# A transformer pair on one core: the opening is reordered around blocks of k, and the gate columns ride with the token-major values

## The chip, the cores and the metric

One core of a Trainium2 chip runs the whole program in one launch. The metric is device microseconds of one execution, the median of several runs; lower is better. The engines are named as the profile names them: PE is TensorE (PEld its weight loads), DVE is VectorE, ACT is ScalarE, POOL is GpSimd, SP issues the DMAs.

## The reference

Two blocks follow each other on 512 tokens of 1024 features. The change lies in the first one, and there ahead of and inside the token mixer (cut):

```python
mod = (silu(c) @ ada_w + ada_b)                       # 6 x 1024
sh_t, sc_t, g_t, sh_c, sc_c, g_c = split(mod, 6)
h = rms_norm(x, tm_pre_g) * (1.0 + sc_t) + sh_t
p = split_columns(h @ w_in)     # ml_q ml_k ml_v ml_o ml_i ml_f gla_q gla_k gla_v gla_r gla_a conf sc gate
ml = mlstm_chunked(p["ml_q"], p["ml_k"], p["ml_v"], p["ml_i"] + ml_i_bias, p["ml_f"] + ml_f_bias)
log_a = log_sigmoid(p["gla_a"] @ gla_w_a2 + gla_a_bias) / 16
gl = gla_chunked(p["gla_q"], p["gla_k"], p["gla_v"], log_a)
a, g = split(p["conf"], 2)      # a convolution branch on a * sigmoid(g)
```

Behind it come the convolution branches, the gates that merge four branches, w_o, a convolutional FFN, and the second block (pooling, sparse attention, FFN). All matrix products are wanted at close to f32 precision.

## The kernel before, in words

**Products.** Features lie on the partitions: x0 and h are 8 k-tiles of 128 x 512. A weight block is 128 x 1024 (8 k-tiles of 128 output columns, 512 KB); `wload` fetches it into a raw tile over SP's queue, ScalarE rounds it to float32r (`hi`, L119) and VectorE takes the rest (`lo`, L120). h is held in the same way as a pair, hh and hl. `mm3` makes one product from three matmuls of 512 columns: hi x hh (L131), hi x hl (L132), lo x hh (L133). A gemm of one block is 24 matmuls into a PSUM bank. `gemm_t` turns the sides round (h is the weight, the weight block the moving side) and gives token-major results: 96 matmuls of 256 columns (L157) for 512 tokens of 256 values. Raw, hi and lo tiles have three buffers each, the stage tiles `sraw` four, PSUM has eight banks (three `acc`, two `tp`, and `pa`, `pb`, `pc`).

**Order.** A scheduler at build time sets a static order on each engine; weight loads are lifted ahead by a fixed priority. Engines wait for each other by semaphores.

**Opening (L353 to L447).** c is fetched as a row broadcast to all partitions (cb). A modulation column is one `ada_st` (L347): VectorE multiplies a 128 x 1024 tile of ada_w with cb and sums it. For k = 0 to 7 the scale column 8+k is made, two pieces of x are loaded, squared (L379) and added (L381), and x times its gain, neither normed nor shifted, is split into hh and hl (L394, L395). With these, four blocks (gq0, gq1, gk0, gk1; tiles `wst`) are multiplied as they arrive. When all x is there, the column sum (L240), the root (`rsqrt`, L217 to L233) and four transposes (L247) give rx, which scales the four results (L411, L413). Then the shift columns 0 to 7 follow, seven by `ada_st` and one by TensorE (L422), and h is made anew, normed and shifted (L428 to L430), for the blocks ifa, ca0, cg0, ca1, cg1. ifa holds the columns of the mLSTM gates and of GLA's rank-16 gate, padded to 128. The missing shift of the first four blocks is made up by sixteen matmuls of the shift columns with `wst` (L439, L440) and four small transposes; it enters as `shw` where gq and gk are scaled (L561, L564).

**GLA and mLSTM.** From ifa the gate rows are made (L480 to L491), then GLA's log gates by two plain f32 products (L540), Exp and Ln and a scan; gv is token-major. kf, the decayed keys, are transposed (L574). For each of two head pairs p: copies of gv into a block-diagonal form (L594, 32 in all), key-value products (L596), state updates one after another on VectorE (L604, L606), copies of the states (L610), the attention products in banks pa and pb (L617) with a predicated copy under the causal mask (L619), and the outputs from attention (L624) and state (L629). The gemms of mq, mk and mv are placed in between by the scheduler. mLSTM follows (gate rows L646 to L676, preparations L700 to L706, products from L713 on), then the transposes of values at L775.

Of the kernel before, what the change touches and what calls it, by code (L numbers as in the profile page):

```python
# [38 lines left out]
for _n, _w in VECS:  # L39
# [6 lines left out]
MT1 = ["gq0", "gq1", "gk0", "gk1", "ifa", "ca0", "cg0", "ca1", "cg1", "gv0", "gv1",  # L46
       "mq0", "mq1", "mk0", "mk1", "mv0", "mv1", "gr0", "gr1", "mo0", "mo1",
       "sb0", "sc0", "sx0", "sb1", "sc1", "sx1"]
NST = 8
NF = 4  # L50
XSTEP = (2, 2, 2, 2, 0, 0, 0, 0)
WSTEP = (1, 1, 1, 1, 1, 1, 1, 1)
ADA_PE = (1,)
# [7 lines left out]
def block_kernel(ctx, tc, io, dbg=None):  # L61
# [83 lines left out]
    def gemm_t(srcs, act, out):  # L145

        kn = KT // len(srcs)
        n = 1024 // kn
        for i, src in enumerate(srcs):
            w = [t.rearrange("p (k n) -> p k n", n=n) for t in wload(src)]  # L150
            for b in range(4):
                t = slice(b * 128, (b + 1) * 128)
                for k in range(kn):
                    q = i * kn + k
                    ah, al = act[0][:, q, t], act[1][:, q, t]
                    for m, (a, x_) in enumerate(((ah, w[0]), (ah, w[1]), (al, w[0]))):
                        T.matmul(out[b], a, x_[:, k], start=(q == 0 and m == 0 and b * n % 512 == 0),  # L157
# [181 lines left out]
    with tc.tile_pool(name="st", bufs=1) as st:  # L339
# [11 lines left out]
        nc.sync.dma_start(out=cb, in_=io["c"].broadcast_to([128, D]))  # L353
        nc.sync.dma_start(out=vec[:, 0:VSTART], in_=io["vec"][:, 0:VSTART])
        A.activation(cb, cb, AF.Silu)
# [4 lines left out]
        wstf = [st.tile([128, NF, 1024], F32R, name=f"wst{n}") for n in range(2)]  # L360
        wst = [(wstf[0][:, m], wstf[1][:, m]) for m in range(NF)]
        wst += [(m4(f"whi{m}", F32R)[:, 0:1024], m4(f"wlo{m}", F32R)[:, 0:1024]) for m in range(NF, NST - 3)]
        accs = [bank(t) for t in ("acc", "acc", "acc", "pa", "pb", "pc", "tp")]
        done = [0] * NST
        ready = 0

        def steps(ms, act, j):
            for m in ms:
                for k in range(done[m], j + 1):
                    sl = slice(k * 128, (k + 1) * 128)  # L370
                    mm3(accs[m], wst[m][0][:, sl], wst[m][1][:, sl], act[0][:, k], act[1][:, k], k == 0, k == KT - 1)
# [1136 lines left out]
```

## Time and profile before

| | |
|---|---|
| median of 3 runs | 1603.59 us (1602.0 to 1603.7) |
| profiled execution | 1603.05 us |
| its span in the trace | 1601.3 us |
| TensorE busy | 1568.9 us (98%) |
| VectorE busy | 1083.4 us (68%) |
| ScalarE busy | 677.5 us (42%) |
| DMA, mean over the span | 110 GB/s, 175.91 MB |

The span is what lies between the first and the last instruction of the trace; the 1.8 us beside it are the start and the end of the execution. Matmuls overlap in the array, so a matmul's own duration (0.39 us for 512 columns) is longer than the time from one start to the next; costs are taken from starts. The granted clock is given as a part of the full 2.4 GHz: 0.50 is 1.2 GHz.

### The profile page before, as it was taken

The page shows a single profiled execution, that of the slowest core. Times are in us where ns is not written, and L with a number is a line of the kernel's source. Part 1 is how long each engine was busy: PE and PEld are TensorE (multiplying, and loading weights), DVE is VectorE, ACT ScalarE, POOL GpSimd, SP SyncE. Part 2 cuts the span into 40 slices and gives each one's busy share as a digit, 9 for nine tenths or more (in the row PEclk, how much of TensorE's full clock was granted, in tenths as well). Part 3 has the DMA queues.
Part 4 walks back from the last instruction along what each step waited for, and adds up shares of the span by engine and source line. Part 5 has one row for each costly group of instructions (what it writes and reads, how often), then busy time and mean ns, then how long its engine had stood idle before and what let it go on. Part 6 is the DMA issues. An engine that isn't in the chain of part 4 may idle for free.

```text
span 1601.3 us, 20852 instructions
## 1 busy us (share of the span) xinstructions
PE 1568.9 (98%) x8015; PEld 1316.4 (82%) x8015; DVE 1083.4 (68%) x2066; ACT 677.5 (42%) x1040; POOL 15.9 (1%) x43
## 2 busy tenths in 40 slices
PE   6999999999999999999999999999999999999997
PEld 4777888888889888888899978888889988888886
DVE  7786897657778865665358899977556565665234
ACT  4456432223463544443244463448343444444122
POOL 0000100000000000000000000000000000000000
PEclk9999999999999999999999999999999999999999
DMA  8411335554550223233345222220241232232331
GB/s 305 170 53 67 106 115 187 184 170 153 177 169 17 79 97 100 92 100 91 96 134 187 75 66 89 83 93 27 79 152 59 80 100 98 92 104 81 98 113 53
DMA packets 50963, 175.91 MB, mean 110 GB/s; under 512 B 5920, under 2 KB 6192, under 8 KB 50864
## 3 DMA queue, kind: packets, MB, share of 16 engines
q1 hardware_dynamic: 50864, 174.58, 33.3%
q8 instruction: 63, 1.03, 0.3%
q14 instruction: 36, 0.29, 0.1%
HBM read 172.46 MB, written 2.10 MB: 109 GB/s over the span
## 4 chain that ended last, share of the span: by engine, by line
PE 90%; DVE 5%; ACT 3%; DMA 1%; issue 1%; SPq 0%; ACTq 0%; DVEq 0%
PE acc L131 23%; PE acc L132 23%; PE acc L133 23%; PE acc L197 3%; PE acc L1340 3%; PE tp L1340 2%; PE pc L1250 1%; PE pa L197 1%; PE pc L197 1%; PE pb L197 1%; PE pb L1340 1%; PE pa L1340 1%; PE pc L1340 1%; DVE lo L120 1%; PE acc L157 1%
## 5 line engine op out<-in xcount | busy, mean ns | idle before, releaser
L120 DVE TENSOR_TENSOR lo<-raw,hi 128x1024 fp32r<-128x1024 f32 (+1 forms) x245 | 296.4, 1211 | 312.0 <-ACT hi L119 307.9
L131 PE MATMUL acc<-hh,hi 128*128 128x512 f32 x1208 | 474.3, 393 | 0.0
L133 PE MATMUL acc<-hh,lo 128*128 128x512 f32 x1208 | 473.1, 392 | 0.0
L132 PE MATMUL acc<-hl,hi 128*128 128x512 f32 x1208 | 473.1, 392 | 0.0
L119 ACT ACTIVATE hi<-raw 128x1024 fp32r<-128x1024 f32 (+1 forms) x245 | 257.1, 1050 | 471.1 <-PE acc L132 352.6
L131 PEld LDWEIGHTS acc<-hh,hi 128*128 128x128 f32 x1208 | 227.7, 189 | 48.9 <-issue 2.0
L132 PEld LDWEIGHTS acc<-hl,hi 128*128 128x128 f32 x1208 | 227.5, 188 | 48.6 <-issue 1.8
L133 PEld LDWEIGHTS acc<-hh,lo 128*128 128x128 f32 x1208 | 227.6, 188 | 47.5 <-issue 0.7
L131 PE MATMUL acc<-act_h,hi 128*128 128x256 f32 (+1 forms) x242 | 80.4, 332 | 0.0
L132 PE MATMUL acc<-act_l,hi 128*128 128x256 f32 (+1 forms) x242 | 80.2, 331 | 0.0
L133 PE MATMUL acc<-act_h,lo 128*128 128x256 f32 (+1 forms) x242 | 80.2, 331 | 0.0
L119 ACT ACTIVATE act_h<-ffe 128x512 fp32r<-128x512 f32 x44 | 27.7, 630 | 102.5 <-DVE ffe L968 102.5
L265 DVE SCALAR_TENSOR_TENSOR raw<-raw,cb 128x1024 f32<-128x1024 f32 x32 | 39.1, 1223 | 40.0 <-DMA raw<-in_ada_dram 40.0
L964 DVE SCALAR_TENSOR_TENSOR ffe<-acc,vec,ffe 128x510 f32<-128x510 f32 x82 | 61.2, 748 | 2.6
L967 ACT ACTIVATE ffe<-ffe 128x512 f32<-128x512 f32 x44 | 27.8, 631 | 79.5 <-DVE ffe L964 79.5
L962 DVE SCALAR_TENSOR_TENSOR ffe<-acc,vec,ffe 128x511 f32<-128x511 f32 x82 | 60.7, 742 | 0.0
L131 PEld LDWEIGHTS acc<-act_h,hi 128*128 128x128 f32 x242 | 46.0, 190 | 4.4
L133 PEld LDWEIGHTS acc<-act_h,lo 128*128 128x128 f32 x242 | 46.0, 190 | 4.3
L132 PEld LDWEIGHTS acc<-act_l,hi 128*128 128x128 f32 x242 | 46.0, 190 | 4.3
L120 DVE TENSOR_TENSOR act_l<-ffe,act_h 128x512 fp32r<-128x512 f32 x44 | 30.3, 690 | 26.5 <-ACT act_h L119 26.5
L808 DVE SCALAR_TENSOR_TENSOR cv<-u,vec,cv 128x512 f32<-128x512 f32 x60 | 43.8, 746 | 0.1
L197 PE MATMUL acc<-hl,hi 128*128 128x256 f32 x144 | 40.2, 285 | 0.0
(632 smaller groups left out, 2778.4 us busy)
## 6 DMA issues: line engine op xcount, KB each, us to landing
raw<-in_up_dram SPq DMA_DIRECT2D x88, 512.0 KB, 3.3
raw<-in_wg_dram SPq DMA_DIRECT2D x48, 512.0 KB, 3.3
raw<-in_dn_dram SPq DMA_DIRECT2D x44, 512.0 KB, 3.5
raw<-in_w_dram SPq DMA_DIRECT2D x43, 512.0 KB, 3.4
raw<-in_ada_dram SPq DMA_DIRECT2D x32, 512.0 KB, 3.4
sraw<-in_ada_dram SPq DMA_DIRECT2D x16, 512.0 KB, 5.3
raw<-in_wo_dram SPq DMA_DIRECT2D x16, 512.0 KB, 3.3
raw<-in_dn_dram SPq DMA_DIRECT2D x11, 384.0 KB, 3.2
```

What stands on the lines that cost most here:

```text
L119: A.activation(hi, src, AF.Copy)
L120: V.tensor_sub(lo, src, hi.bitcast(F32))
L131: T.matmul(out, wh_, ah, start=start, stop=False)
L132: T.matmul(out, wh_, al, start=False, stop=False)
L133: T.matmul(out, wl_, ah, start=False, stop=stop)
L197: T.matmul(a, w_, x_, start=(k == 0 and n == 0 and half == 0), stop=(k == KT - 1 and n == 2 and half == 1), skip_group_check=True)
L265: V.scalar_tensor_tensor(raw, raw, 1.0, cb, op0=ALU.mult, op1=ALU.mult, accum_out=mod[:, i:i + 1])
L808: V.scalar_tensor_tensor(cv[:, j], u0[:, j, k:k + 512], htap[:, 2 * k + j:2 * k + j + 1], cv[:, j], op0=ALU.mult, op1=ALU.add)
L962: V.scalar_tensor_tensor(t[:, 1:512], acc[:, 0:511], vcol(taps, 44 + i), t[:, 1:512], op0=ALU.mult, op1=ALU.add)
L964: V.scalar_tensor_tensor(t[:, 2:512], acc[:, 0:510], vcol(taps, i), t[:, 2:512], op0=ALU.mult, op1=ALU.add)
L967: A.activation(e[0], e[0], AF.Silu)
L1340: T.matmul(o, act[a][:, k, t], w[:, n0:n1], start=(k == 0 and i == 0), stop=(k == KF - 1 and i == 2), skip_group_check=True)
```

## The change

All of x is loaded first. cb is made on the chip: the silu of c as eight columns, each spread by a transpose. Matmuls without a use (`warm`) stand ahead of the first product. rx is made before any product. Then a single loop runs over k: it makes the scale and the shift column of that k, h of that k, and fetches one weight block that holds the k-tile of eight column blocks (gq0, gq1, gk0, gk1, ca0, cg0, ca1, cg1), each with a PSUM bank of its own. No shift is repaired later. The ifa block is gone: its 24 columns stand behind the 256 of gv, so `gemm_t` now has 280 columns, and the gate columns are copied out (gt4) and transposed. The gates' Exp and Ln run once over 128 x 1536. mq and mk are computed ahead of GLA. In GLA both value copies of a group stand ahead of its products, the attention products alternate between the halves of the array's rows, and the outputs are written as two loops.

```diff
-MT1 = ["gq0", "gq1", "gk0", "gk1", "ifa", "ca0", "cg0", "ca1", "cg1", "gv0", "gv1",
+MT1 = ["gq0", "gq1", "gk0", "gk1", "ca0", "cg0", "ca1", "cg1", "mq0", "mq1", "mk0", "mk1", "mv0", "mv1",
...
+NGV = 280
+WW = 1120
+WARM = (3, 12)
...
+        for j in range(KT):
+            nc.sync.dma_start(out=x0[:, j], in_=io["xT"][:, j])
+
+        zero = st.tile([128, 256], F32, name="zero")
+        G.memset(zero, 0.0)
+        idle = bank("acc")
+
+        def warm(n, x_):
+            for _ in range(n):
+                T.matmul(idle[:, 0:x_.shape[1]], ident if x_ is not zero else zero[:, 0:128], x_, start=True, stop=True)
+
+        warm(WARM[0], zero)
...
+        for n in range(2):
+            cp = bank(("pb", "pc")[n])
+            for k in range(4):
+                T.transpose(cp[:, k * 128:(k + 1) * 128], ccol[:, 4 * n + k:4 * n + k + 1].to_broadcast([128, 128]), ident)
...
+        warm(WARM[1], zero)
...
+        colsum(pc, [ssx])
+        warm(2, ssx)
+        V.tensor_copy(s0, pc[:, 0:4])
+        rx = st.tile([128, 512], F32, name="rx")
+        A.activation(rx, rowcast(rsqrt(s0, 1.0 / D, 4)), AF.Copy)
+        warm(2, rx)
+
+        accs = [bank(t) for t in ("acc", "acc", "acc", "pc", "pa", "pb", "tp", "tp")]
         for j in range(KT):
+            g, sh = gcols[:, 0, j:j + 1], mod[:, j:j + 1]
             ada_st(8 + j)
+            ada_st(j)
+            floor[0] = tc.cur_priority
+            w = wload(io["w1"][j])
...
+            V.scalar_tensor_tensor(t, x0[:, j], g, rx, op0=ALU.mult, op1=ALU.mult)
             A.activation(h[0][:, j], t, AF.Identity, bias=sh)
             V.scalar_tensor_tensor(h[1][:, j], t, sh, h[0][:, j].bitcast(F32), op0=ALU.add, op1=ALU.subtract)
...
+            for m in range(NST):
+                sl = slice(m * 128, (m + 1) * 128)
+                mm3(accs[m], w[0][:, sl], w[1][:, sl], h[0][:, j], h[1][:, j], j == 0, j == KT - 1)
...
+        out = [bank(t) for t in ("acc", "acc", "acc", "pc")]
+        gemm_t([io["wgv"][n] for n in range(2)], h, [o[:, 0:NGV] for o in out], NGV)
+        for b in range(4):
+            V.tensor_copy(gt4[:, b, 0:64].rearrange("p (g c) -> p g c", c=32)[:, :, 0:4],
+                          out[b][:, 256:264].rearrange("p (g c) -> p g c", c=4))
+            V.tensor_copy(gt4[:, b, 64:80], out[b][:, 264:280])
+            A.activation(gv[:, b], out[b][:, 0:256], AF.Copy)
+        ifa = bank("tp")
+        for b in range(4):
+            T.transpose(ifa[0:80, b * 128:(b + 1) * 128], gt4[:, b], ident)
...
+        A.activation(rows[:, 2:5], rows[:, 2:5], AF.Exp, scale=-1.0)
+        A.activation(rows[:, 2:5], rows[:, 2:5], AF.Ln, bias=1.0)
...
+        for dst, nm in ((mq, "mq"), (mk, "mk")):
+            for j in range(2):
+                A.activation(dst[:, j], acc_of(f"{nm}{j}"), AF.Copy)
...
+            atp = [bank("pa"), bank("pb")]
+            for b in range(4):
+                t = slice(b * 128, (b + 1) * 128)
+                for hh in range(2):
+                    r = slice(64 * hh, 64 * hh + 64)
+                    T.matmul(atp[hh][:, t], gk[r, p, t], gq[r, p, t])
```

Where the instructions stand now is seen in the orders. First TensorE's queue at the very start. Before, it begins with products (`wst_109` and `wst_110` are the hi and lo halves of the first weight blocks):

```order
L131 MATMUL acc<-hh,wst_109 128x512
L132 MATMUL acc<-hl,wst_109 128x512
L133 MATMUL acc<-hh,wst_110 128x512
```

And now (`zero`, `ssx` and `rx` as moving or weight side mark the matmuls without a use; `cst` is the identity or the ones; L237 is the column sum, L244 the transposes that spread rx):

```order
L358 MATMUL acc<-zero 128x256 x5
L369 MATMUL pb<-cst,ccol 128x128 x4
L369 MATMUL pc<-cst,ccol 128x128 x4
L358 MATMUL acc<-zero 128x256 x10
L237 MATMUL tp<-cst,ssx 128x1 x4
L358 MATMUL acc<-ssx,cst 128x512 x2
L244 MATMUL tp<-cst,rs_y 128x128 x4
L358 MATMUL acc<-rx,cst 128x512 x2
L129 MATMUL acc<-hh,hi 128x512 x3
```

The products moved behind the column sum and the spread of rx, and fifteen zero matmuls and the spread of c stand ahead of those.

Next VectorE's queue in the changed kernel at the same place (L381 adds the squares, L371 copies half of cb, L385 takes the column sum, L344 is `ada_st`, L214 to L230 are the root, L118 is lo, L400 and L402 are nt and hl):

```order
L371 COPY cb<-pc 128x512
L381 TENSOR_TENSOR ssx<-ssx,sq 128x512 x6
L385 COPY s_90<-tp 128x4
L344 SCALAR_TENSOR_TENSOR sraw,mod<-sraw,cb 128x1024
L214 TENSOR_SCALAR rs_s<-s_90 128x4
L397 SCALAR_TENSOR_TENSOR gcols<-mod,scb_120,vec 128x1
L215 TENSOR_SCALAR rs_i<-rs_s 128x4
L216 TENSOR_SCALAR rs_y<-rs_i 128x4
L344 SCALAR_TENSOR_TENSOR sraw,mod<-sraw,cb 128x1024
L228 TENSOR_TENSOR rs_u<-rs_y 128x4
```

The first two modulation sums stand inside the root of rx; before, the first of them stood at the head of the queue and the root came after four of them.

Last TensorE's queue where GLA begins. Before (L617 attention, L574 transposes of kf, L596 key-value products; L131 to L133 are gemms of mq and mk):

```order
L617 MATMUL pa<-e_97 128x128 x4
L617 MATMUL pb<-e_97 128x128
L574 MATMUL tp<-cst,e_97 128x128 x4
L617 MATMUL pb<-e_97 128x128 x3
L133 MATMUL acc<-hh,lo 128x512
L574 MATMUL tp<-cst,e_97 128x128 x4
L596 MATMUL pc<-x1a,e_97 64x256 x2
L131 MATMUL acc<-hh,hi 128x512
L132 MATMUL acc<-hl,hi 128x512
```

And now (L548 transposes of kf, L590 attention, L569 key-value products, L154 the token-major gemm of mv):

```order
L548 MATMUL tp<-cst,e_97 128x128 x8
L590 MATMUL pa<-e_97 128x128
L590 MATMUL pb<-e_97 128x128
L590 MATMUL pa<-e_97 128x128
L590 MATMUL pb<-e_97 128x128
L590 MATMUL pa<-e_97 128x128
L569 MATMUL pc<-x1a,e_97 64x256 x4
L590 MATMUL pb<-e_97 128x128
L590 MATMUL pa<-e_97 128x128
L590 MATMUL pb<-e_97 128x128
L154 MATMUL acc<-hi,hh 128x256
```

Both transposes now stand ahead of the first attention product, and what is mixed with GLA is the gemm of mv alone; those of mq and mk stand ahead of L548.

## Rows read from the trace of the kernel before

**Rows 1.** The page: TensorE's row of the busy times (busy us, share of the span, instructions), and the chain of work that ended last, by engine.

```profile
PE 1568.9 (98%) x8015; PEld 1316.4 (82%) x8015; DVE 1083.4 (68%) x2066; ACT 677.5 (42%) x1040; POOL 15.9 (1%) x43
...
PE 90%; DVE 5%; ACT 3%; DMA 1%; issue 1%; SPq 0%; ACTq 0%; DVEq 0%
```

**Rows 2.** The table by stage, core 0. Columns: the stretch in us from the span's start, its length, busy us and instructions of each engine, the granted TensorE clock as a part of full speed (PEclk), the DMA engines' busy share and GB/s. (The clock's record begins at 20.0 us.)

```profile
11.46:20.10 8.64, 6.58 (x12) 3.55 (x12) 8.27 (x13) 4.88 (x8) 0.00 (x0) 1.00 1.04 403
...
97.80:101.90 4.10, 1.78 (x15) 1.39 (x14) 4.10 (x9) 3.25 (x7) 0.00 (x0) 1.00 0.36 128
101.90:108.70 6.80, 6.80 (x24) 4.18 (x23) 5.24 (x15) 1.19 (x2) 0.00 (x0) 0.50 0.23 77
...
141.50:197.70 56.20, 55.80 (x347) 49.57 (x343) 46.52 (x92) 35.81 (x80) 5.60 (x16) 1.00 0.30 98
197.70:250.00 52.30, 52.30 (x235) 43.29 (x235) 52.05 (x82) 17.28 (x23) 0.00 (x0) 1.00 0.41 130
```

**Rows 3.** The timeline of the opening, VectorE and TensorE: start us, us, engine, line, operation, out<-in, shapes, count, and in brackets the idle time of the engine before it with what ended it.

```profile
5.25 0.17 DVE L359 TENSOR_SCALAR scb<-vec 128x8 f32<-128x8 f32 x1 [5.25 <-DMA vec<-in_vec_dram]
...
7.64 1.23 DVE L347 SCALAR_TENSOR_TENSOR sraw<-sraw,cb 128x1024 f32<-128x1024 f32 x1 [2.22 <-DMA sraw<-in_ada_dram]
...
8.79 0.08 DVE L347 DVE_READ_ACCUMULATOR sraw<-sraw,cb 128x1 f32 x1
...
11.46 0.80 PE L131 MATMUL acc<-hh,wst 128*128 128x512 f32 x1 [11.46 <-ACT wst L119]
```

**Rows 4.** The timeline of TensorE, same columns: 512-column matmuls of the opening and of a later stretch. The distance between the starts is what one costs.

```profile
17.16 0.63 PE L131 MATMUL acc<-hh,wst 128*128 128x512 f32 x1
...
19.29 0.63 PE L133 MATMUL acc<-hh,wst 128*128 128x512 f32 x1
...
53.66 0.39 PE L131 MATMUL acc<-hh,hi 128*128 128x512 f32 x1
...
69.08 0.39 PE L133 MATMUL acc<-hh,lo 128*128 128x512 f32 x1
```

**Rows 5.** The timeline of TensorE, same columns: the column sum, the shift column made by TensorE, the first shift repair matmul and the first row behind the sixteen, the two products of the gate factor, the first of the 96 token-major matmuls and the first row behind them.

```profile
25.03 1.02 PE L240 MATMUL tp<-cst,ssx 128*128 128x1 f32 x8 [0.77 <-DVE ssx L381]
...
44.43 1.84 PE L422 MATMUL tp<-ccol,sraw 128*128 128x1 f32 x16
...
69.30 0.40 PE L439 MATMUL tp<-wst,sh 128*2 128x512 f32 x1
...
72.98 0.39 PE L131 MATMUL acc<-hh,hi 128*128 128x512 f32 x1
...
79.08 1.98 PE L540 MATMUL tp<-rows,wa 16*128 16x512 f32 x4
80.99 0.39 PE L157 MATMUL acc<-hi,hh 128*128 128x256 f32 x1
...
92.61 0.40 PE L131 MATMUL acc<-hh,hi 128*128 128x512 f32 x1
```

**Rows 6.** Groups of instructions by line and shape, VectorE from 0 to 70 us and then ScalarE from 0 to 160 us: line, engine, operation, names, shapes, count | busy us, mean ns of one | idle before them and what ended it.

```profile
L347 DVE SCALAR_TENSOR_TENSOR sraw<-sraw,cb 128x1024 f32<-128x1024 f32 x15 | 18.3, 1219 | 2.2 <-DMA sraw<-in_ada_dram 2.2
L120 DVE TENSOR_TENSOR lo<-raw,hi 128x1024 fp32r<-128x1024 f32 x5 | 6.0, 1221 | 3.9 <-ACT hi L119 3.9
L430 DVE SCALAR_TENSOR_TENSOR hl<-nt,mod,hh 128x512 fp32r<-128x512 f32 x8 | 6.0, 750 | 0.8 <-ACT hh L429 0.8
...
L232 DVE SCALAR_TENSOR_TENSOR rs_u<-rs_u,rs_s 128x4 f32<-128x4 f32 x3 | 0.5, 158 | 0.0
...
L119 ACT ACTIVATE hi<-raw 128x1024 fp32r<-128x1024 f32 x15 | 15.7, 1052 | 25.2 <-PE acc L132 16.6 <-DMA raw<-in_w_dram 4.9 <-PE pc L132 3.4
L429 ACT ACTIVATE hh<-nt,mod 128x512 fp32r<-128x512 f32 x8 | 5.8, 723 | 10.9 <-DVE nt L428 10.3 <-DVE sh L120 0.5
...
L610 ACT ACTIVATE x1a<-x1a 64x960 f32<-64x960 f32 x4 | 4.0, 1003 | 1.3 <-DVE x1a L606 1.2
```

**Rows 7.** The same view, VectorE from 100 to 160 us: the state updates of GLA, the copies of its values (one of 32 stands before 100) and the predicated copies of one of its two halves.

```profile
L606 DVE SCALAR_TENSOR_TENSOR x1a<-x1a,fcol,pc 128x64 f32<-128x64 f32 x28 | 7.8, 278 | 1.4 <-PE pc L596 0.8
...
L594 DVE COPY x1a<-gv 32x128 f32<-32x128 f32 x31 | 6.8, 218 | 2.5 <-PE pc L596 1.8
...
L619 DVE COPY_PREDICATED x2a<-x2a,pa 128x512 f32<-128x512 int32 x2 | 1.5, 739 | 0.9 <-PE tp L624 0.9
```

**Rows 8.** The timeline, columns as in Rows 3: the first of the mLSTM gate rows on VectorE and the row behind the last; the first key-value matmuls of GLA, its last run of outputs and the first row behind it; the last preparation for mLSTM on ScalarE; the first row behind the values of mLSTM; the first transposes of the values of the gated branches.

```profile
83.94 1.36 DVE L646 TENSOR_TENSOR_SCAN rows<-x2a,rows 4x128 f32<-4x128 f32 x4
...
91.42 1.21 DVE L120 TENSOR_TENSOR lo<-raw,hi 128x1024 fp32r<-128x1024 f32 x1
...
105.31 1.12 PE L596 MATMUL pc<-x1a,e 128*64 128x256 f32 x4
...
138.30 0.42 PE L629 MATMUL tp<-x1a,e 128*32 128x128 f32 x6
...
141.48 0.50 PE L132 MATMUL acc<-hl,hi 128*128 128x512 f32 x1
...
154.39 0.62 ACT L706 ACTIVATE mql<-mql 64x512 fp32r<-64x512 f32 x1
...
154.25 0.40 PE L713 MATMUL pc<-mx,sel 128*128 128x512 f32 x1
...
197.72 0.98 PE L775 MATMUL tp<-cst,mv 128*128 128x128 f32 x7
```

More of the change, by code (lines that the diff above doesn't have):

```diff
@@ L156, in gemm_t @@
                     for m, (a, x_) in enumerate(((ah, w[0]), (ah, w[1]), (al, w[0]))):
-                        T.matmul(out[b], a, x_[:, k], start=(q == 0 and m == 0 and b * n % 512 == 0),
+                        T.matmul(out[b], a, x_[:, k], start=(q == 0 and m == 0 and b % (512 // n) == 0),
                                  stop=(q == KT - 1 and m == 2), skip_group_check=True)
@@ L429, in block_kernel @@
             A.activation(h[0][:, j], t, AF.Identity, bias=sh)
             V.scalar_tensor_tensor(h[1][:, j], t, sh, h[0][:, j].bitcast(F32), op0=ALU.add, op1=ALU.subtract)
-            if j not in (KT - 3, KT - 2):
-                steps(range(NF, NST), h, j)
-        shs = sm.tile([128, KT, 2], F32R, tag="sh", name="sh", bufs=1)
-        split(shs[:, :, 0], shs[:, :, 1], mod[:, 0:KT])
-        shp = bank("tp")
-        for j in range(KT):
-            wk = [wstf[n].rearrange("p m (k c) -> p m k c", k=KT)[:, :, j] for n in range(2)]
-            T.matmul(shp[0:2], shs[:, j], wk[0], start=(j == 0), stop=False, skip_group_check=True)
-            T.matmul(shp[0:1], shs[:, j, 0:1], wk[1], start=False, stop=(j == KT - 1), skip_group_check=True)
@@ L441, in block_kernel @@
-        shr = st.tile([128, 512], F32, tag="nt", name="shr", bufs=2)[0:2]
-        A.activation(shr, shp[0:2], AF.Copy)
-        tp = bank("tp")
-        for m in range(NF):
-            T.transpose(tp[:, 2 * m:2 * m + 2], shr[:, m * 128:(m + 1) * 128], ident[0:2, 0:2])
-        shw = sm.tile([128, NF], F32, tag="shw", name="shw", bufs=1)
-        V.tensor_reduce(shw, tp[:, 0:2 * NF].rearrange("p (m n) -> p m n", n=2), axis=AX.X, op=ALU.add)
+            if j == 4:
+                load_consts()
@@ new lines, in block_kernel @@
+        ifa = bank("tp")
+        for b in range(4):
+            T.transpose(ifa[0:80, b * 128:(b + 1) * 128], gt4[:, b], ident)
+        gx, fm, fa = (rows[:, n] for n in range(3))
+        gf = gx[32:36]
+        i_sb, b_sb, d_sb = (rows[0:4, n] for n in range(3))
+        fb = vec[32:36, VOFF["if_bias"]:VOFF["if_bias"] + 1]
+        A.activation(gx[64:80], ifa[64:80], AF.Copy)
+        A.activation(fa[32:36], ifa[32:36], AF.Abs, bias=fb)
+        V.tensor_scalar(gf, ifa[32:36], fb, 0.0, op0=ALU.add, op1=ALU.min)
@@ new lines, in block_kernel @@
+        A.activation(i_sb, ifa[0:4], AF.Identity, bias=vec[0:4, VOFF["if_bias"]:VOFF["if_bias"] + 1])
+        gab = rows[:, 3:5]
+        gmn = m4("gmn")[:, 0:1024].rearrange("p (j t) -> p j t", j=2)
+        for j in range(2):
+            u = bank(("pa", "pb")[j])
+            T.matmul(u, wa2[64:80, j * 128:(j + 1) * 128], gx[64:80])
+            A.activation(gab[:, j], u, AF.Abs, bias=vcol("gla_a_bias", j))
+            V.tensor_scalar(gmn[:, j], u, vcol("gla_a_bias", j), 0.0, op0=ALU.add, op1=ALU.min)
@@ L625, in block_kernel @@
                              start=(b == 0 and hh == 0), stop=False, skip_group_check=True)
+            for b in range(4):
                 for c in range(4):
@@ L1169, in block_kernel @@
         pump(PUMP_V0)
-        gemm_t([io["w2"][m + n] for n in range(4)], h, vb)
+        gemm_t([io["w2"][m + n] for n in range(4)], h, vb, 512)
         for b in range(4):
```

191 lines of the change are left out of this document (50 added, 141 removed).

## The prediction

> **What bounds the kernel now.** I first read the page's busy times and its chain of waits: TensorE is busy for 98% of the span and carries 90% of the chain [rows 1]. The reader should see that almost any TensorE work taken out, or any TensorE gap closed, is time won, and that nothing else is. Next I read the table by stage [rows 2], because a mean hides the stage that is changed. From 141.5 to 197.7 TensorE is busy for 55.80 of 56.20 us and afterwards without a break; VectorE is nearly full from 197.7 to 250 (52.05 of 52.30) but there TensorE still never waits. Before 141.5 there are holes: the first product starts at 11.46 [rows 3], 2.3 us are idle between 97.8 and 101.9, and from 101.90 the granted clock is 0.50 for 6.80 us. Last I read single TensorE rows for the rate [rows 4]: 68 intervals from 53.66 to 69.08 give 0.227 us per 512-column matmul at the full clock, five from 17.16 to 19.29 give 0.426. So the opening runs at half rate; the clock column shows 1.00 there, but the pitch says 1.2 GHz, and I trust the pitch.
>
> The place where both kernels can be compared is the first of the transposes at L775, at 197.72 [rows 8]. Behind it the two orders are the same on every engine, except that the changed kernel has already issued seven 512-column matmuls (7 x 0.227 = 1.6 us) that the old one still has before it. I therefore work out when the changed kernel gets there.
>
> **The change, part by part.**
>
> *Work removed and added on TensorE* [rows 5]. The ifa block goes: 24 x 0.227 = 5.4 us. The shift repair at L439/L440 goes: 69.30 to 72.98, 3.7. L422's sixteen matmuls go: 1.8. The gate columns now ride with the token-major values: the old 96 matmuls of 256 columns took 11.62 us (80.99 to 92.61), 0.121 each. 280 columns are not in the trace; from below they cost 0.121, from above 280/512 of a slower pitch, say 0.14; between 256 columns at 0.121 and 512 at 0.227 the line gives 0.131, and I take 0.130: 96 x 0.130 = 12.5, 0.9 more than now. Four transposes of the gate columns add 0.5. Net 9.5 us less work. The rest of the sum is waiting.
>
> *Opening.* Now products start at 11.46 on an x that is normed later. In the changed order no product starts before the norm factor rx. TensorE issues five zero matmuls, eight transposes of c, ten zero matmuls, then the column sum. Plain f32 is not float32r: two 16x512 products at L540 took 1.91 us [rows 5], so 0.24 per pass of 512 columns and some 0.48 for a 256-column zero matmul, twice that at half rate. Five at half rate from about 1.3 and ten at full rate, with the transposes between them, end at about 12.1; if the clock stays low for longer, at 15.8. vec lands at 5.2 [rows 3]; behind it cst, eight x pieces (2 MB), two ada tiles and a weight tile (1.5 MB) stream at 403 GB/s [rows 2]: x complete near 9, ada 8 at 10.3, ada 0 at 11.6, weights at 12.9. The transfers are then ahead of TensorE's queue. Column sum 1.0 (L240, [rows 5]): 13.1. VectorE then has ada 8 (1.2), twelve small steps of the root (0.16 each, 0.20 apart since each needs the last), ada 0 between them (1.2) [rows 6]: 17.9. Four transposes and the copy of rx: 19.4, where TensorE does its two rx matmuls (1.9) while it would wait anyway. Then lo, ada and nt are queued: nt ends at 21.0, hh takes 0.72 [rows 6], and the first product is at **21.8**. Bounds: 20.0 if ada 8 lies beside the column sum and lo beside the root, 25.5 if the zero matmuls run at half rate. Between 13 and 20 TensorE does little; the old kernel shows 0.50 after such a hole (101.90, [rows 2]), where 6.80 us cost 3.4. I charge 1.5, bounds 0 and 4.
>
> The Trainium skill (TensorE: Matmul & The Clock Gate, Part 1 and Part 4) says that the throttled state is the default, that activity releases it, and that transposes do not count as activity in the same way. The half pitch until 19.29 agrees with the first half of that; no row separates the second. By it the column sum and the rx transposes would bridge nothing, and the loop would pay nearer the upper bound of 4 than my 1.5, which would make the sum some 1593.
>
> *The loop over k.* Eight steps of 24 matmuls: 192 x 0.227 = 43.6. VectorE needs per step two ada sums and one lo (1.22 each), nt and hl (0.75 each, taken alike) and 0.3 of small ones: 5.4 by durations [rows 6], but the next instruction starts before one ends (an ada sum of 1.23 begun at 7.64 is followed at 8.79, [rows 3]), so with 0.08 less for each of the five 5.0 us against TensorE's 5.4; the transfers need 1.5 MB / 403 GB/s = 3.9. All lie beside it, with 0.4 us to spare a step; if the overlaps fail, VectorE paces the loop at about the same 5.4. ScalarE has hi 1.05 and hh 0.72 [rows 6]. Loop end: 21.8 + 43.6 + 1.5 = 66.9.
>
> *Values, gates, mq and mk.* 12.5 + 0.7 (transposes and a short wait) + 1.9 (the two L540 products) + 96 x 0.227 = 21.8 for mq and mk, which stand ahead of GLA now: 103.8. The gate chain on ScalarE and VectorE (table loads, one wide Exp and Ln, scans, four products) starts at 82 and gives the second kf near 102.5 by its rows' durations, so it hides behind mq/mk with 1.3 us to spare. If it slips, TensorE waits as it did before 101.9.
>
> *GLA.* The old kernel spread mq, mk and their products through GLA; now only the 96 matmuls of mv (11.5) remain to fill it. From the first L596 at 105.31 to the last L629 at 141.48 the old one took 36.2 us [rows 8]. In the new order VectorE, after kf, first does the mLSTM gate rows, which took 7.5 us (83.94 to 91.42, [rows 8]): it is free at about 109.3 for the 32 value copies (7.0), 28 state updates (7.8) with two first copies at much the same price (0.5), four predicated copies (3.0) and two lo (2.4) [rows 6, 7], plus an estimated 0.03 between 62 short ones (1.9): 22.5, so 131.8. Exposed behind it: one L596 group 1.0 [rows 8], the sd copy 1.0, and the output's last matmuls 3.2 (138.30 to 141.48). GLA ends at 137.0. Own work in these 33.2 us is about 27.5, so 5.7 are waits. I add 1.0 for a stretch at half clock, since 101.90 to 108.70 cost 3.4 where GLA began with waits: **138.0**. Bounds 133 (waits halved) and 144 (the old 36.2 from about 108).
>
> *mLSTM up to the transposes.* The old kernel still had mk and mv from 141.48 to 154.25 and then 43.5 us to 197.72 [rows 8]. The new one has only those 43.5, the seven matmuls (1.6), and a wait: ScalarE's sixteen preparations of mq and mk, 0.62 each, or 10 us, had mv as their cover and the last of them stands at 154.39 [rows 8]; that cover is gone. Most can now start inside GLA, since mq and mk are there at 104, and I estimate 2.2 left (bounds 0 and 8). 138.0 + 43.5 + 1.6 + 2.2 = 185.3.
>
> **Sum.** 197.72 - 185.3 = 12.4 us earlier. Behind L775 TensorE was never idle up to 250 [rows 2], so it carries the whole gain to the end if weights come as early as now. The profiled execution took 1603.05, within 0.6 of the median 1603.59: 1603.05 - 12.4 = **1590.6**.
>
> **Rivals.**
> *GLA uncovered.* The old chain's 36.2 us stay although the filler is gone: end 144 instead of 138, gain 6.4, 1596.7. For it: each of the four L596 groups waits for VectorE's copies, and the updates wait for it. Against it: part of the old 36.2 was gemm work put in between. 20%.
> *Late opening.* Zero matmuls at half rate: first product 25.5, gain 8.7, 1594.4. For it: the old opening stays at half rate for 8 us. 10%.
> *Few stalls.* Opening at 20.0 (1.8), no clock loss (1.5 + 1.0), GLA waits halved (2.9), no mLSTM wait (2.2): 9.4 more, gain 21.8, 1581.3. 20%.
> *Given back.* VectorE, with 52.05 of 52.30 busy from 197.7 to 250, paces the weights when TensorE arrives 12 us sooner with the same list behind it: about 1603. Against it: TensorE has no idle time there now, and the list is only shifted as a whole. 6%.
> *Slower.* TensorE stays at the lower clock in the k loop because each step waits for hh or hl a little, as in the old opening. A step at 0.426 costs 24 x 0.199 = 4.8 us more. Beyond 12.4/4.8 = 2.6 steps the kernel loses, at four of the eight it takes 12.4 - 19.1 = 6.7 us longer, 1609.8. For it: 0.4 us of VectorE's slack a step is little. Against it: once the old kernel ran without gaps (53.66 on) it kept the full rate. 6%. The Trainium skill has this pattern in the same page's section "HAM oscillation — how this bites in real kernels": a loop whose steps each end in a wait starts each step throttled.
>
> **How the numbers follow.** The forecast itself, 1586 to 1595, has 38%. A measurement can tell about 0.2%, 3.2 us. The four faster cases hold 88%, from which I take 2 for a GLA that eats all: faster 0.86; same 0.07 (given back, and that); slower 0.07 (the clock, and some unseen wait). Below 1580 lie about 8% (few stalls, all bounds), above 1600 about 12%: the range is 1580 to 1600.
>
> **What would show it.** First L129 product near 21.8 at a pitch of 0.227; loop end near 67 with 24 matmuls in 5.4 us; 280 columns at 0.130; kf before mk ends; the last L602 near 138; the first L748 transpose near 185. A granted clock of 0.5 in the loop, a gap ahead of L548 or a GLA beyond 144 would make the prediction wrong, and so would a stretch behind L748 that is longer than the old one from L775.

## The result, and the profile after

The change made the kernel slower: 1624.26 us (1623.31 to 1625.27) against 1603.55 for the kernel before on the same chip, a ratio of 1.0142 [1.013, 1.0154]. The forecast was 1590.6, with 1600 as its upper end.

The page of the changed kernel, the rows that answer to [rows 1]:

```profile
PE 1592.1 (98%) x8005; PEld 1325.4 (82%) x8005; DVE 1077.3 (66%) x2060; ACT 666.9 (41%) x1027; POOL 17.2 (1%) x46
...
PE 92%; DVE 5%; ACT 2%; issue 1%; DMA 0%; SPq 0%; ACTq 0%; DVEq 0%
```

TensorE has ten instructions less than before and is busy for 23.2 us more. So the loss is not a wait: the same instructions take longer. The timeline of TensorE after the change (columns as in [rows 3]): the matmuls on rx that have no use and the first product behind them, the first token-major matmuls, the product of the gate factor, the kf transposes, a wait in GLA, the last run of GLA's outputs and the row behind it, a wait in the tail of mLSTM, the transposes of the values of the gated branches, the last product. (A plain f32 matmul stands in the trace as two: the two on rx show as x4.)

```profile
20.71 3.68 PE L358 MATMUL acc<-rx,cst 128*128 128x512 f32 x4 [0.69 <-ACT rx L387]
23.43 1.64 PE L129 MATMUL acc<-hh,hi 128*128 128x512 f32 x3
...
68.73 0.29 PE L154 MATMUL acc<-hi,hh 128*128 128x280 f32 x1
68.86 0.29 PE L154 MATMUL acc<-lo,hh 128*128 128x280 f32 x1
...
83.33 1.12 PE L487 MATMUL pa<-rows,wa 16*128 16x512 f32 x2
...
105.99 1.04 PE L548 MATMUL tp<-cst,e 128*128 128x128 f32 x8
...
116.05 0.44 PE L596 MATMUL tp<-gv,x2a 128*128 128x64 f32 x2 [4.07 <-DVE x2a L592]
...
143.69 1.07 PE L602 MATMUL tp<-x1a,e 128*32 128x128 f32 x30
144.69 0.50 PE L686 MATMUL pc<-mx,sel 128*128 128x512 f32 x1
...
185.21 0.80 PE L129 MATMUL acc<-hh,hi 128*128 128x512 f32 x1 [6.25 <-ACT tmp L734]
...
187.93 0.46 PE L129 MATMUL acc<-hh,hi 128*128 128x512 f32 x1
...
196.80 1.09 PE L748 MATMUL tp<-cst,mv 128*128 128x128 f32 x8 [0.96 <-DVE mv L726]
...
1613.32 0.39 PE L1313 MATMUL tp<-hi,act_l 128*128 128x512 f32 x1
```

The last product in the trace of the kernel before:

```profile
1592.75 0.39 PE L1340 MATMUL tp<-hi,act_l 128*128 128x512 f32 x1
```

At the transposes the change is 0.9 us ahead (196.80 against 197.72 [rows 8]), though it has seven products more behind them than the old kernel; at the last product it is 20.6 us behind. The table by stage shows what happens in between, in a stretch where both do nothing but 512-column products at full clock. First the kernel before, then the changed one, with three of its early stages (columns as in [rows 2]):

```profile
560.00:740.00 180.00, 180.00 (x796) 149.05 (x795) 110.94 (x135) 74.82 (x99) 0.00 (x0) 1.00 0.30 96
```

```profile
23.00:67.00 44.00, 44.00 (x187) 35.22 (x186) 36.73 (x71) 16.32 (x22) 3.92 (x11) 0.99 0.70 241
...
116.00:132.00 16.00, 15.95 (x76) 13.45 (x76) 6.90 (x23) 2.00 (x2) 0.00 (x0) 0.57 0.00 0
...
175.00:200.00 25.00, 17.79 (x85) 14.36 (x85) 24.44 (x50) 9.38 (x16) 0.00 (x0) 0.86 0.40 127
560.00:740.00 180.00, 180.00 (x778) 146.38 (x777) 108.81 (x132) 72.76 (x97) 0.00 (x0) 1.00 0.28 94
```

In the same 180 us, without an idle moment and with a granted clock of 1.00 in both, TensorE issues 778 products instead of 796: 0.2314 us each instead of 0.2261, from one start to the next (the pitch of the texts below). The page counts 3 x 1216 such products; times 0.0053 that is 19.3 us, nearly all of the loss. The other rows show two more things: a half clock in GLA (0.57) behind a wait of 4.1 us, and a wait of 6.3 us before 185.21.

**A line of the diff that the prediction did not price** explains the rate: `WW = 1120`. To hold the block of 280 columns, raw, hi and lo became 4480 bytes wide in each partition instead of 4096, and they stay so for the whole program. 4480 is not a multiple of 256. The compiled programs place the tiles at these bytes of a partition (remainders modulo 256 in brackets):

```
         before                               after
hi       23520 27616 31712   (224 224 224)    24576 29056 33536   (  0 128   0)
lo       35808 39904 44000   (224 224 224)    38016 42496 46976   (128   0 128)
hh, hl   48096, 64480        (224, 224)       51456, 67840        (  0,   0)
```

hi and lo are the weight side of a product, hh and hl its moving side. Before, all agree modulo 256; after, some weight tiles lie 128 bytes off. Theory A: a product costs more where its two sides disagree. Its rivals: wider tiles cost by their width, or the new order behind L748 is slower of itself.

### The profile page after: what moved, and what is told of

Read it like the earlier page. It is cut to its first block, busy times and chain, and to the rows that moved or that the text cites. A ratio compares the mean times of both kernels' runs of the same rounds, so it can differ in the third digit from the quotient of the medians.

```text
span 1621.6 us, 20813 instructions
## 1 busy us (share of the span) xinstructions
PE 1592.1 (98%) x8005; PEld 1325.4 (82%) x8005; DVE 1077.3 (66%) x2060; ACT 666.9 (41%) x1027; POOL 17.2 (1%) x46
## 4 chain that ended last, share of the span: by engine, by line
PE 92%; DVE 5%; ACT 2%; issue 1%; DMA 0%; SPq 0%; ACTq 0%; DVEq 0%
PE acc L130 23%; PE acc L131 23%; PE acc L129 22%; PE acc L194 3%; PE acc L1313 3%; PE acc L154 2%; PE tp L1313 2%; PE pc L1223 1%; PE pa L194 1%; PE pc L194 1%; PE pb L194 1%; PE pa L1313 1%; PE pc L1313 1%; PE pb L1313 1%; DVE lo L118 1%
## 5 line engine op out<-in xcount | busy, mean ns | idle before, releaser
L118 DVE TENSOR_TENSOR lo<-raw,hi 128x1024 fp32r<-128x1024 f32 (+2 forms) x249 | 301.6, 1212 | 353.1 <-ACT hi L117 348.1
L131 PE MATMUL acc<-hh,lo 128*128 128x512 f32 x1216 | 483.7, 398 | 0.0
L130 PE MATMUL acc<-hl,hi 128*128 128x512 f32 x1216 | 482.4, 397 | 0.0
L117 ACT ACTIVATE hi<-raw 128x1024 fp32r<-128x1024 f32 (+2 forms) x249 | 261.4, 1050 | 481.1 <-PE acc L130 334.1
L129 PEld LDWEIGHTS acc<-hh,hi 128*128 128x128 f32 x1216 | 231.7, 191 | 60.5 <-ACT tmp L734 6.6
L131 PEld LDWEIGHTS acc<-hh,lo 128*128 128x128 f32 x1216 | 228.7, 188 | 49.9 <-issue 0.2
L131 PE MATMUL acc<-act_h,lo 128*128 128x256 f32 (+1 forms) x242 | 81.0, 335 | 0.0
L131 PEld LDWEIGHTS acc<-act_h,lo 128*128 128x128 f32 x242 | 45.6, 188 | 4.5
L118 DVE TENSOR_TENSOR act_l<-ffe,act_h 128x512 fp32r<-128x512 f32 x44 | 30.4, 690 | 26.6 <-ACT act_h L117 26.6
L194 PE MATMUL acc<-hl,hi 128*128 128x256 f32 x144 | 40.2, 284 | 0.0
```

Source lines behind the costliest of these rows:

```text
L117: A.activation(hi, src, AF.Copy)
L118: V.tensor_sub(lo, src, hi.bitcast(F32))
L129: T.matmul(out, wh_, ah, start=start, stop=False)
L130: T.matmul(out, wh_, al, start=False, stop=False)
L131: T.matmul(out, wl_, ah, start=False, stop=stop)
L194: T.matmul(a, w_, x_, start=(k == 0 and n == 0 and half == 0), stop=(k == KT - 1 and n == 2 and half == 1), skip_group_check=True)
```

## Experiments

**Addresses mended, the change otherwise whole.**

```diff
-WW = 1120
+WW = 1152
```

(The weight block in memory keeps its 1120 columns.) 1152 columns are 4608 bytes, 18 x 256. Here and below the second time, and what a ratio refers to, is the kernel before on the same chip.

> The changed kernel with one number altered: raw, hi and lo tiles 1152 wide instead of 1120, so 4608 bytes a partition instead of 4480; the order on every engine is the same. Theory A (address step): in the changed kernel a hi, lo or activation tile no longer starts at the same place modulo 256 bytes as its partners, and each 512-column matmul then costs 0.232 instead of 0.227 us; at 4608 bytes all tiles agree again, some 5,300 matmuls get 4.5 ns back, and the time falls from 1624.3 to 1599, the pitch of hi x hl to 0.227. Theory B (the reordered opening or the longer activity slows TensorE for the rest): time stays near 1624, pitch 0.232.

Measured: 1603.33 against 1601.36, 1.0014 [1.0005, 1.0024]. The table by stage and the timeline of TensorE in this kernel:

```profile
116.00:132.00 16.00, 16.00 (x96) 13.34 (x99) 6.85 (x28) 2.00 (x2) 0.00 (x0) 0.63 0.00 1
...
560.00:740.00 180.00, 180.00 (x796) 149.05 (x795) 110.96 (x135) 74.84 (x99) 0.00 (x0) 1.00 0.29 96
```

```profile
66.91 0.29 PE L154 MATMUL acc<-hi,hh 128*128 128x280 f32 x1
...
81.48 1.12 PE L487 MATMUL pa<-rows,wa 16*128 16x512 f32 x2
...
103.70 1.03 PE L548 MATMUL tp<-cst,e 128*128 128x128 f32 x8
...
142.87 0.50 PE L686 MATMUL pc<-mx,sel 128*128 128x512 f32 x1
...
183.37 0.79 PE L129 MATMUL acc<-hh,hi 128*128 128x512 f32 x1 [6.24 <-ACT tmp L734]
...
189.08 0.46 PE L130 MATMUL acc<-hl,hi 128*128 128x512 f32 x1
...
195.13 1.09 PE L748 MATMUL tp<-cst,mv 128*128 128x128 f32 x8
```

The 796 products are back, and with them some 20.5 us of the 25 expected (1.0142 to 1.0014): width alone costs nothing, since these tiles are wider still. What remains is that the change gains nothing where 12.4 us were forecast. That is a second question, taken up below.

**The kernel before, with the address spoiled or kept in three ways.** Tiles of 4480 bytes; 128 bytes put between the weight tiles and the activations; tiles of 4352 bytes, which is 17 x 256 and so agrees modulo 256 but not modulo 512.

```diff
-        raw = wr.tile([128, 1024], F32, tag="raw", name="raw")
+        raw = wr.tile([128, 1120], F32, tag="raw", name="raw")
...
-            hi = wh.tile([128, 1024], F32R, tag="hi", name="hi")[:, :n]
-            lo = wl.tile([128, 1024], F32R, tag="lo", name="lo")[:, :n]
+            hi = wh.tile([128, 1120], F32R, tag="hi", name="hi")[:, :n]
+            lo = wl.tile([128, 1120], F32R, tag="lo", name="lo")[:, :n]
```

```diff
+    padp = ctx.enter_context(tc.tile_pool(name="padp", bufs=1))
+    pad = padp.tile([128, 32], F32, name="pad")
...
+    G.memset(pad, 0.0)
```

The third is the first diff with 1088 for 1120.

> The kernel before with nothing but raw, hi and lo tiles of 1120 instead of 1024 columns (the added columns are never used); the order on every engine is the same. Theory A: 1626.5 (23 us more), pitch of hi x hl to lo x hh 0.2325, of lo x hh to the next 0.234. Theory B: 1603.5, pitch 0.227.

> The kernel before with an unused tile of 128 bytes a partition between the lo pool and the activations, so that weights agree among themselves but lie 128 bytes off the moving tile, modulo 256. Theory A in the form that weights and moving tile must agree: all 512-column matmuls at 0.2325 to 0.234, some 30 us more, 1633. Theory A2, that only the step from one weight tile to the next counts: no change, 1603.5.

> The kernel before with raw, hi and lo tiles of 1088 columns (4352 bytes: the same modulo 256, not modulo 512), order unchanged. Theory A with 256 bytes: 1603.5, pitch 0.227. If the step that counts is 512 bytes or more: some 20 us slower.

Measured: 1.0132 [1.0111, 1.0152], 1.0129 [1.0108, 1.0149] and 0.9998 [0.9988, 1.0008]. The stage row of the first, the second and the third:

```profile
560.00:740.00 180.00, 180.00 (x777) 146.44 (x776) 106.50 (x128) 73.91 (x98) 0.00 (x0) 1.00 0.28 94
```

```profile
560.00:740.00 180.00, 180.00 (x776) 145.94 (x775) 106.81 (x129) 73.28 (x98) 0.00 (x0) 1.00 0.29 95
```

```profile
560.00:740.00 180.00, 180.00 (x796) 149.05 (x795) 110.41 (x133) 75.39 (x100) 0.00 (x0) 1.00 0.30 97
```

The old order with the new width loses what the change lost. With the 128 bytes between, all weight tiles still agree with each other, and it costs as much: what counts is that they agree with the moving side. The shift by a multiple of 256 is free. I had expected more of the second than it cost, since products of the changed kernel between sides 128 off stood 233.6 ns apart; here the mean is 180/776 = 0.2320 us.

The mixed placing of the changed kernel costs as much, though fewer than half of its products have sides that disagree. The single products show how the cost is spread. Sorted by the tiles that the compiled program gives each product, its 180 us show 0.2267 us only for hi x hh with hi and hh alike and the same hi behind it (173 products). Where a product's own two sides agree but the weight tile of the product behind it lies 128 bytes off, it takes 0.2325 (173 of hi x hl) or 0.2350 (75 of lo x hh), as much as where its own sides disagree (0.2329 to 0.2341 in the three large groups). So a misplaced tile also seems to cost the product ahead of it; no run moved one tile alone.

**64 bytes between.** The second diff with 16 for 32, in the kernel before.

> The kernel before with an unused tile of 64 bytes a partition (instead of 128) between the lo pool and the activations; order unchanged. If what counts is whether weights and moving tile agree modulo 128 or 256: as slow as with 128 bytes, 1622, pitch 0.2325. If only the half of 256 in which a tile starts counts: 64 bytes leave part of the pairs alike and the pitch lies at 0.227, 1602.

Measured: 1.0057 [1.0041, 1.0073], and in the table by stage:

```profile
560.00:740.00 180.00, 180.00 (x788) 147.69 (x787) 109.26 (x132) 74.84 (x99) 0.00 (x0) 1.00 0.29 96
```

0.2284 us per product, between 0.2261 and 0.2320, and the time lies between the two that were foretold. So it isn't a matter of agreeing or not. Nor is it the distance alone: in this stretch hi x hh takes 0.2259, hi x hl 0.2291 and lo x hh 0.2317, though the sides lie 64 bytes apart in all three.

**Where the forecast gain went: the tail of mLSTM.** With the addresses mended, TensorE still waits 6.2 us before 183.37 for a bank that ScalarE must read (L733, L734). What TensorE waited for longest in that kernel, and ScalarE's timeline ahead of the read:

```profile
PE acc L129 <- ACT tmp L734: 6.2, 1, 6.2
PE tp L596 <- DVE x2a L592: 4.4, 1, 4.4
```

```profile
180.86 1.15 ACT L722 ACTIVATE tmp<-num 128x512 f32<-128x512 f32 x2 [3.31 <-DVE num L718]
181.91 0.58 ACT L733 ACTIVATE tmp<-acc 128x512 f32<-128x512 f32 x1
182.72 0.60 ACT L734 ACTIVATE tmp<-acc 128x512 f32<-128x512 f32 x1 [0.23 <-DVE ss L723]
```

On ScalarE's queue the squares of the mLSTM norm (L722) stand ahead of the reads of the gr banks, and wait for VectorE. The edit moves the block of GLA's gates, which reads the two gr banks, ahead of the norm:

```diff
+        gla = bo()
+        for j in range(2):
+            r = acc_of(f"gr{j}")
...
         rd = sm.tile([128, 16], F32, tag="rd", name="rd")
...
-        gla = bo()
-        for j in range(2):
-            r = acc_of(f"gr{j}")
...
```

> The changed kernel with tiles of 1152 (the run with that one number altered stands 0.14% above before) and one block of code moved: the GLA gate (reads of gr0 and gr1 from PSUM, their tanh and product) stands ahead of the mLSTM norm instead of behind it. In that run TensorE waited 6.2 us near 179 for ScalarE to read gr0 out of its bank, and ran at half clock behind the wait. Theory S (a queue order: ScalarE's read stands behind a square that waits for VectorE): the wait goes, with its 1.7 us of lost clock; 7 us faster, ratio to before 0.997. Rival F (TensorE has run out of independent gemms there, since mq, mk and others were placed earlier): the wait moves to the next bank or to the transposes of the mLSTM values, ratio stays 1.001.

Measured: 1593.61 against 1602.02, 0.9951 [0.9934, 0.9967], 0.63 points below the kernel with mended addresses. The stage of the wait:

```profile
175.00:200.00 25.00, 25.00 (x124) 21.10 (x123) 24.17 (x49) 8.95 (x14) 0.72 (x1) 1.00 0.51 168
```

TensorE is busy throughout, at the full clock, where the changed kernel had 17.79 of 25.00 at 0.86. The wait cost what it lasted and the half clock behind it.

**GLA's inner loops as before, or mq and mk behind GLA.** Two undoings, each on top of the mended addresses. First the value copies one by one, the attention products one bank after the other, the outputs in one loop; then mq and mk put back.

```diff
-            atp = [bank("pa"), bank("pb")]
-            for b in range(4):
-                t = slice(b * 128, (b + 1) * 128)
-                for hh in range(2):
...
+                atp = bank(("pa", "pb")[hh])
+                for b in range(4):
+                    t = slice(b * 128, (b + 1) * 128)
```

```diff
-        for dst, nm in ((mq, "mq"), (mk, "mk")):
-            for j in range(2):
-                A.activation(dst[:, j], acc_of(f"{nm}{j}"), AF.Copy)
...
+        for dst, nm in ((mq, "mq"), (mk, "mk")):
+            for j in range(2):
+                A.activation(dst[:, j], acc_of(f"{nm}{j}"), AF.Copy)
```

> The changed kernel with tiles of 1152 and the three edits inside GLA undone (value copies and products by turns, attention products half by half, attention and state outputs in one loop); mq and mk stay ahead. In the run with 1152 alone TensorE waited 4.4 us near 112 for the predicated copies and ran at half clock for some 13 us behind. Theory L (the split output loop puts the attention outputs, and so the wait, ahead of the key-value products): wait and clock loss shrink, 5 to 8 us faster, ratio 0.997. Rival F (too little filler: only mv's gemm stands in GLA): the wait stays or moves, ratio 1.001 to 1.003.

> The changed kernel with tiles of 1152 and the gemms of mq and mk written behind GLA again, as in the kernel before; all else as changed. Rival F (filler): TensorE has more to do inside GLA, the wait near 112 and the half clock behind it go, 5 to 8 us faster, ratio 0.997. Theory L: the wait stays, since it hangs on the order of GLA's own instructions and the order shows little gemm work between them; ratio 1.001 or above.

Measured: 0.9975 [0.9965, 0.9984] and 0.997 [0.9957, 0.9983]. Of the first, three stages, and what TensorE waited for longest (engine, tile, line, what it waited for: us, times, longest):

```profile
106.00:116.00 10.00, 6.78 (x45) 5.47 (x43) 9.73 (x35) 3.15 (x5) 0.00 (x0) 0.83 0.33 107
116.00:132.00 16.00, 15.57 (x126) 12.78 (x125) 11.13 (x42) 3.03 (x4) 0.00 (x0) 0.89 0.00 1
...
175.00:200.00 25.00, 19.88 (x86) 15.94 (x86) 25.00 (x49) 11.64 (x18) 0.00 (x0) 0.93 0.44 141
```

```profile
PE acc L129 <- ACT tmp L732: 4.0, 1, 4.0
PE tp L595 <- DVE x2a L590: 3.2, 1, 3.2
```

The waits of the second:

```profile
PE pc L565 <- DVE rs_y L230: 3.9, 1, 3.9
PE pa L586 <- DVE e L534: 2.9, 1, 2.9
PE pc L565 <- DVE x1a L575: 2.7, 1, 2.7
```

With the old loops the clock from 106 to 132 is 0.87 (0.83, then 0.89) instead of 0.74 (0.91, then 0.63), and the two waits are shorter. So the three edits of GLA's loops, taken together, were a loss. With mq and mk behind GLA there are three waits inside GLA, 9.5 us in all, and none in the tail. Its 0.997 is what rival F foretold, and the wait for the predicated copies (x2a) did go, but these three came in its place; in sum it is the tail's wait that went. Each theory has one run on its side, so the order of the loops and the lack of filler are not told apart here.

**Without the matmuls that have no use.** `WARM = (0, 0)` and no `warm` behind the column sum and rx, addresses mended.

> The changed kernel with tiles of 1152 and without the matmuls that have no use (zeros, and those on ssx and rx). If they keep the clock up, the first products now run at 0.426 us each for some 8 us and it is 2 to 4 us slower, ratio 1.003. If they do not (in the changed kernel the rx ones themselves ran at half rate and held the first product back by 0.4 us), no change or 0.5 us faster, ratio 1.001.

Measured: 1.0016 [1.0007, 1.0026], the same as with them. The timeline of TensorE at the first product, with the thirteen products up to 30.22:

```profile
24.51 1.65 PE L129 MATMUL acc<-hh,hi 128*128 128x512 f32 x3 [2.59 <-ACT hh L399]
...
27.66 0.63 PE L130 MATMUL acc<-hl,hi 128*128 128x512 f32 x1
...
30.22 0.40 PE L130 MATMUL pc<-hl,hi 128*128 128x512 f32 x1
```

From 27.66 six products take 2.56 us, 0.427 each: the half rate lasts to 30.22, and no such stretch is in the kernel with mended addresses. It is not seen in the medians. The profiled opening itself varies by as much: in the seven kernels here that have the whole opening with mended addresses the first token-major matmul starts between 66.2 and 69.6, in the one without these matmuls at 70.8.

**The opening and the gate columns alone**, both undoings together.

> Only the new opening and the gate columns behind gv, with tiles of 1152: mq and mk behind GLA and GLA's loops are both as in the kernel before. If the opening is worth the 12 us that the start of the token-major product shows (67 against 81) and GLA behaves as before: 1590 on a chip where before takes 1602, ratio 0.993. If an earlier GLA waits for its gate chain and for VectorE whatever its own order, as in the run with mq and mk put back (10 us of waits): ratio 0.997.

Measured: 1605.17 against 1601.56, 1.0022 [1.0012, 1.0031], slower than both foretold ratios. Three stages of GLA, and the two longest waits of TensorE:

```profile
106.00:116.00 10.00, 9.65 (x42) 5.80 (x41) 5.41 (x21) 1.56 (x3) 0.00 (x0) 0.69 0.01 2
116.00:132.00 16.00, 9.91 (x62) 6.02 (x62) 13.00 (x54) 3.11 (x4) 0.00 (x0) 0.59 0.09 33
132.00:145.00 13.00, 11.40 (x69) 7.81 (x70) 5.27 (x24) 4.76 (x8) 0.00 (x0) 0.76 0.01 1
```

```profile
PE pc L563 <- DVE x1a L573: 4.5, 2, 3.9
PE pa L584 <- DVE e L534: 2.9, 1, 2.9
```

The opening that reaches its end some 12 us sooner (69.39 against 80.99) gains nothing alone. GLA takes it back in waits and half clock, and the product of the gate factor, at 83.96, is no sooner than the old 79.08 [rows 5] (next section).

**The best of them: mended addresses, GLA's old loops, the gr banks read early.** And, as a counterpart, mq and mk behind GLA with the gr banks read early, where no tail wait was left to remove.

> Tiles of 1152, GLA's three inner edits undone, and the reads of gr0 and gr1 ahead of the mLSTM norm; mq and mk stay ahead of GLA. If the two waits (GLA, tail) are separate and both orders remove their own: 0.9975 less the 4.0 us of the tail wait that was left, and its clock: 0.9945, below both single runs. If the time that one wait gives back is taken by the other: 0.997.

> Tiles of 1152, mq and mk behind GLA, and the reads of gr0 and gr1 ahead of the mLSTM norm. With mq and mk behind GLA the tail wait was gone already, so the second edit has nothing left to remove: 0.997, the same as with mq and mk put back alone. If it helps otherwise: 0.992.

Measured: 1590.53 against 1601.56, 0.9931 [0.9917, 0.9946]; and 0.9972 [0.9959, 0.9985], as good as without the early reads. The first beats what was foretold for it, the second is as foretold. The stages of the first:

```profile
106.00:116.00 10.00, 6.77 (x33) 6.19 (x32) 8.98 (x29) 0.63 (x1) 0.00 (x0) 0.70 0.16 55
116.00:132.00 16.00, 15.58 (x134) 12.25 (x134) 11.08 (x42) 3.66 (x4) 0.00 (x0) 0.98 0.01 2
...
175.00:200.00 25.00, 25.00 (x117) 20.72 (x117) 24.57 (x47) 7.95 (x12) 0.00 (x0) 1.00 0.47 160
```

This version beats both kernels, by 11.0 us the one before. That its time is the forecast one is chance: it holds edits that the change does not.

## Why the prediction was wrong

The sum is compared with the kernel with mended addresses, whose rows show the change without the slower rate.

**The step that failed** is "Behind L775 TensorE was never idle up to 250, so it carries the whole gain to the end". The order and the clock behind L748 were as I had put them; the price of a product was not. I took 0.227 us for a 512-column product [rows 4] as a constant and priced what the diff does with instructions, not what `WW` does to where tiles lie. Of the 1.42% that the kernel lost, 1.28 go when the addresses are mended. That is not all: with mended addresses it takes 1603.33, still above the range, because two more terms of the sum failed, the clock in GLA and the wait in mLSTM (below). The list of what would make the forecast wrong named the symptom, a longer stretch behind L748, without a cause for it and without a case in the sum.

Of this the Trainium skill (SBUF — State Buffer, section "Operand start alignment") says that an operand must start at a multiple of its element size, and of that rule: "This is about legality, not speed". All these tiles keep it; the runs show a price of 1.3% beside it.

**Opening and loop: right at the end, in part by luck.** First product at 23.26 for 21.8, loop end at 66.91 for 66.9. The 1.5 us for a slow clock weren't needed (192 products in 43.65 us, 0.227 each), and the first product came that much later: two errors of 1.5 that cancel by chance. Nor did the loop pay the upper bound of 4. In the changed kernel it was TensorE itself that was late: the useless matmuls on rx took from 20.71 to 23.43, not the 1.9 of the sum. The rival *late opening* lay at 25.5. The rival *slower* by the clock in the loop didn't come: 44.00 of 44.00 us busy at 0.99. The pattern of the Trainium skill that I had set beside it (TensorE: Matmul & The Clock Gate, "HAM oscillation — how this bites in real kernels") needs steps that end in a wait, and there were none, so no run here tests it.

**280 columns: right.** 0.13 each (68.73 to 68.86; 0.129 on average over the 96).

**mq and mk ahead of GLA: right.** kf's transposes at 103.70 for 103.8, and the gate chain did hide behind mq and mk. But before, those transposes stood at 101.48, so GLA begins later than it did:

```profile
101.48 0.75 PE L574 MATMUL tp<-cst,e 128*128 128x128 f32 x4
```

The gate factor's product is at 81.48, where the old one was at 79.08 [rows 5], because the gate columns now come with the values and no longer from a block of their own ahead of them. So nothing of the 14 us gained by 66.91 (80.99 before) passes the gates as such; it is in the 21.8 us of products done ahead, and counts only if GLA and mLSTM, with less to fill them, don't wait in their place. All of the forecast gain hung on the next two terms.

**GLA: the clock mis-sized.** From the transposes to its end 39.2 us (103.70 to 142.87) for 34.2. The rival *GLA uncovered*, which ends at 144, had 40.2 from there and was nearer. The waits were smaller than the 5.7 of the sum: 4.4. But I charged 1.0 us for the clock. The stage from 116 to 132 has 0.63 granted over 16 us without idle time, 16 x 0.37 = 5.9 us, and the 0.91 from 106 to 116 adds 0.9. In the old kernel 6.80 us at 0.50 cost 3.4 [rows 2]; I took a third of that without a row to say why.

**mLSTM: a wait that I did not see.** From there to L748 52.3 us for 45.7 (43.5 and 2.2; the seven products do not belong here, see below). The cover of the preparations wasn't it. It is ScalarE's order: the read of the gr banks stands behind squares that wait for VectorE, 6.2 us, and 2.8 more at half rate behind it (13 products in 5.71 us, 183.37 to 189.08, for 13 x 0.227 = 2.95). I had named bounds of 0 and 8 for this term, for another reason. Taking the wait away gave 0.63 points.

**Slips.** I wrote that the changed kernel has done seven more products when it reaches L748. It is the reverse: they come behind it (7045 rows of TensorE from there on, 7038 in the old kernel). By that premise the sum should have ended at a gain of 14.0, since the old kernel would still have had them to do; as they lie, 1.6 us moves behind L748, and 12.4 stands, with 183.7 at L748. Two sums of the working don't come out either. 2 MB at 403 GB/s are 5.2 us, so behind 5.2 x is complete at 10.4 and not near 9; the first product does not hang on it. And 102.5 + 7.5 is 110.0, not 109.3, which would put GLA's end 0.7 later.

The sum again, with the measured terms: 0.1 sooner, 5.0 and 6.6 later, 195.2 at L748 for 195.13 measured; 197.72 - 195.13 - 1.6 = 1.0 us of gain left. The trace agrees (its last product, at 1591.57, is 1.2 us ahead of the old one's), but it is that of the fastest of ten executions (1601.67 to 1605.69). The medians say 2.0 us slower, and the interval of the ratio lies above 1. What makes up the difference I leave open.

## What to carry to other kernels

A tile's width can be part of the price of every product that reads the tile, because it decides where the tiles behind it lie. Before widening a shared buffer, look where it and all behind it come to lie, and keep the weight and the moving side alike modulo 256 bytes; the padding that did it here cost nothing that was measured. Work done sooner counts only if the next stage's inputs are sooner too: look for the product that the stage begins with and compare its time, before adding up what was won ahead of it. When an engine that only copies banks out has a waiting instruction ahead of a copy, the products can wait for it; here moving that copy up gave 0.63 points.

## What the hardware showed that I had not expected

f32 products of 512 columns took on average 0.2261 us with the two sides' start addresses alike modulo 256 bytes, 0.2284 with 64 bytes between, 0.2320 with 128, at a granted clock of 1.00 in each case, and tiles 4352 bytes wide, 17 x 256, changed nothing. A product between agreeing sides took 0.2325 or 0.2350 when the weight tile of the next one lay 128 bytes off. Why was not found out.

After idle times of a similar length the half clock lasted very differently: after 4.1 us in GLA, with products of 64 and 128 columns behind it, the stage from 116 to 132 has 0.57 in the changed kernel; after 6.3 us in the tail, with 512-column products behind it, the half rate ended at 187.93, 2.7 us on. In the kernel with mended addresses the same tail wait, 6.2 us, was followed by 5.7 us of half rate. With the old order of GLA's loops and a wait of 3.2 us the stage from 116 to 132 had 0.98 in the best kernel and 0.89 in the other, but the stage before it 0.70 and 0.83: over both stages it is 0.87 in either. Neither the length of the wait nor what follows it was varied alone, so what makes the half clock last is open.
